# Bidirectional recurrence: score tiles side by side in PSUM, five double-width masked copies, diagonal products over 128 rows, keys on GpSimd

## The chip, the core and the metric

One Trainium2 chip, one of its cores, one launch. The metric is device time in microseconds of that core. Three timed runs of the kernel before gave 2304.19, 2304.97 and 4443.5 us; the median, 2304.97 us, is what a changed kernel is set against. The profile is of one further execution, which took 2300.62 us.

## What is computed

Two layers of a hybrid trunk over 512 latent tokens and 256 context tokens, width 1024. Each layer is a norm, one wide input projection, four token mixers, a gated merge, an output projection and an MLP. The change touches only the fourth mixer, a bidirectional gated recurrence (HGRN2) with 4 heads of 64 keys and 64 values. In one direction:

```python
def step(S, xs):                       # one chunk
    qc, kc, fc, ic = xs
    b = jnp.cumsum(fc, axis=2)         # running log decay
    diff = b[:, :, :, None, :] - b[:, :, None, :, :]
    dec = jnp.where(lower_tri, jnp.exp(jnp.minimum(diff, 0.0)), 0.0)
    a = jnp.einsum('bhtd,bhsd,bhtsd->bhts', qc, kc, dec)
    o = jnp.einsum('bhts,bhsv->bhtv', a, ic) + jnp.einsum('bhtd,bhdv->bhtv', qc * jnp.exp(b), S)
    return advance(S, b, kc, ic), o
```

It is run forwards and, on flipped tokens, backwards, and both results are added. Layer 0 needs it for all 768 tokens, layer 1 for the 512 latent tokens.

## The kernel before

Everything is written once in Python and put in order by a scheduler that knows priorities and its own cost of each instruction. The result is one fixed list of instructions for each engine, run in that order: an engine whose next instruction is not ready waits, whatever stands behind it.

Most of the time is dense work: a 128-row weight unit is loaded by DMA, split into a high and a low part (line 69 on ScalarE, `whi`; line 70 on VectorE, `wlo`), and multiplied in three products (lines 88, 89, 91, `big<-hhi,whi` and so on).

The recurrence works feature-major: the 64 keys of a head lie on partitions 0 to 63 for the forward direction and on 64 to 127 for the backward one, tokens along the free axis, in chunks of 128 tokens. `hg_state` (lines 438 to 479) makes the state of each chunk: decayed keys `hke`, a transpose on TensorE (line 457), a product with the values (line 463), and a running update `hs` on VectorE (line 477).

`hg_out` (from line 481) makes the outputs for two tiles of 128 tokens at a time; here such a pair of tiles is called a granule. Layer 0 has 4 heads x 3 granules, layer 1 has 4 x 2, so 20 granules in all. One granule is:

- `hE` (four VectorE subtractions, then two passes of ScalarE over 1024 columns): the decay to a reference point at four block sizes `LEVELS` of 64, 32, 16 and 8 tokens.
- `hKL`, the keys times `hE` for each level (line 503; levels 0 and 1 on GpSimd, 2 and 3 on VectorE), and `hQ`, the queries times `hE`, one VectorE instruction over 1024 columns.
- `hd`, `hem`, `hec`: the decay inside blocks of 8 tokens, times the queries (`hd`) and keys (`hem`), and the decay from the chunk's start, times the queries (`hec`).
- for each of the two tiles: four score products (line 525) over 128 rows, and two diagonal products over 64 rows each, the forward direction on rows 0 to 63 (line 526), the backward one on rows 64 to 127 (line 527). They land in two PSUM tiles (`sm`), and six masked copies on VectorE (lines 531 and 532, 128x128 each) put them together into two matrices A1 and A2 (`hA`).
- for each of the two tiles three output products (line 542): the state times `hec`, the values times A1, the values times A2. The two tiles use the two column halves of the array (`tile_position=(0, 64 * j)`), then ScalarE copies the output out (line 544).

`self.fill(n)` draws dense work (a quarter of a gate unit a time) from a generator, so that TensorE has something to do between the steps of a granule. PSUM tiles named `sm` rotate through four buffers, `hKL` and the pairs of `hA` through two each.

Of the kernel before, what the change touches and what calls it, by code (L numbers as in the profile page):

```python
# [8 lines left out]
F32 = mybir.dt.float32  # L9
# [4 lines left out]
AF = mybir.ActivationFunctionType  # L14
ALU = mybir.AluOpType
# [4 lines left out]
P = 128  # L20
# [30 lines left out]
class K:  # L51
# [429 lines left out]
    def hg_out(self, hd, S, grans, o, p, p2):  # L481
        nc = self.nc
        k, c, q = self.hk[hd], self.hc[hd], self.hq[hd]
        r0 = 64 * (hd % 2)
        G = 256
        for g in grans:
            a = g * G
            cs, qs_, ks = c[:, a:a + G], q[:, a:a + G], k[:, a:a + G]
            E = p.tile([P, 4, G], F32, name="hE")
            QL = p2.tile([P, 4, G], F32, name="hQ")  # L490
            for n, H in enumerate(LEVELS):
                nb = G // (2 * H)
                cv = cs.rearrange("p (b s) -> p b s", s=2 * H)
                self.tt(E[:, n].rearrange("p (b s) -> p b s", s=2 * H), cv,
                        cv[:, :, H:H + 1].to_broadcast([P, nb, 2 * H]), ALU.subtract)
            self.act(E, E, AF.Abs)
            self.act(E, E, AF.Exp, scale=-1.0)
            KL = self.hKL[self.kl_i % 2]
            self.kl_i += 1
            for n, H in enumerate(LEVELS):  # L500
                v = lambda t: t.rearrange("p (b s) -> p b s", s=2 * H)
                for lo_, hi_, h0 in ((0, 64, 0), (64, 128, H)):
                    (nc.vector if n >= 2 else nc.gpsimd).tensor_tensor(v(KL[lo_:hi_, n])[:, :, h0:h0 + H], v(ks)[lo_:hi_, :, h0:h0 + H],
                            v(E[lo_:hi_, n])[:, :, h0:h0 + H], ALU.mult)
            self.tt(QL, E, qs_[:, None, :].to_broadcast([P, 4, G]), ALU.mult)
            d = p2.tile([P, G], F32, name="hd")
            em = p2.tile([P, G], F32, name="hem")
            ec = p2.tile([P, G], F32, name="hec")
            self.fill(1)
            c8 = cs.rearrange("p (b s) -> p b s", s=8)  # L510
            self.tt(d.rearrange("p (b s) -> p b s", s=8), c8, c8[:, :, 4:5].to_broadcast([P, G // 8, 8]), ALU.subtract)
            self.act(em, d, AF.Exp, scale=-1.0)
            self.act(d, d, AF.Exp)
            self.act(ec, cs, AF.Exp)
            self.tt(d, d, qs_, ALU.mult)
            self.tt(em, em, ks, ALU.mult)
            self.tt(ec, ec, qs_, ALU.mult)
            sets = []
            for j in range(2):
                s = slice(j * P, (j + 1) * P)  # L520
                pa = self.p_sm.tile([P, 512], F32, name="sm")
                pb = self.p_sm.tile([P, 512], F32, name="sm")
                dst = [pa[:, 0:128], pa[:, 128:256], pa[:, 256:384], pb[:, 0:128], pa[:, 384:512], pb[:, 128:256]]
                for n in range(4):
                    nc.tensor.matmul(dst[n], KL[:, n, s], QL[:, n, s], start=True, stop=True)  # L525
                nc.tensor.matmul(dst[4], em[0:64, s], d[0:64, s], start=True, stop=True)
                nc.tensor.matmul(dst[5], em[64:128, s], d[64:128, s], start=True, stop=True)
                A1, A2 = self.hA[self.a_i % 2]
                self.a_i += 1
                for n in range(5):  # L530
                    nc.vector.copy_predicated(A1, self.masks[:, n], dst[n])
                nc.vector.copy_predicated(A2, self.masks[:, 5], dst[5])
                sets.append((A1, A2))

            self.fill(1)
            po = self.p_sm.tile([P, 512], F32, name="sm")
            for n in range(3):
                for j in range(2):
                    t = 2 * g + j
                    iv = self.hi_[:, t, hd * 64:hd * 64 + 64]  # L540
                    w, x = ((S[:, t], ec[:, j * P:(j + 1) * P]), (iv, sets[j][0]), (iv, sets[j][1]))[n]
                    nc.tensor.matmul(po[64 * j:64 * j + 64, 0:P], w, x, start=n == 0, stop=n == 2, tile_position=(0, 64 * j))  # L542
            for j in range(2):
                nc.scalar.copy(o[r0:r0 + 64, a + j * P:a + (j + 1) * P], po[64 * j:64 * j + 64, 0:P])

    def hg_begin(self, p, p1):
        nc = self.nc
        self.hk, self.hc, self.hq = {}, {}, {}
        self.kl_i = self.a_i = 0
        self.smask = p.tile([P, 384], U8, name="smask")  # L550
        m32 = p1.tile([P, T], F32, name="hge")[:, :384]
        nc.scalar.dma_start(m32, self.io["smask"])
        nc.vector.tensor_copy(self.smask, m32)
        self.hKL = [p.tile([P, 4, 256], F32, name=f"hKL{i}") for i in range(2)]
        self.hA = [[p.tile([P, P], F32, name=f"hA{i}{j}") for j in range(2)] for i in range(2)]
        for t in self.hKL:
            nc.gpsimd.memset(t, 0.0)
        for x in self.hA:
            for t in x:
                nc.gpsimd.memset(t, 0.0)  # L560
# [988 lines left out]
```

## Time and profile before

| | |
|---|---|
| median of three timed runs | 2304.97 us |
| the profiled execution | 2300.62 us |
| span from its first to its last instruction | 2298.8 us |
| TensorE matmul busy | 2232.7 us (97%) |
| VectorE busy | 1487.9 us (65%) |
| ScalarE busy | 940.7 us (41%) |
| GpSimd busy | 171.1 us (7%) |

An engine counts as busy from the start of an instruction to its end. Matmuls overlap: one that begins every 0.11 us is recorded with 0.27 us, so for TensorE the distance between two starts tells what a product costs, and the idle time in front of one tells what it waited for. A 4-byte product is recorded as two passes, so eight products of line 525 stand as x16.

### The profile page before, as it was taken

The page shows a single profiled execution, that of the slowest core. Times are in us where ns is not written, and L with a number is a line of the kernel's source. Part 1 is how long each engine was busy: PE and PEld are TensorE (multiplying, and loading weights), DVE is VectorE, ACT ScalarE, POOL GpSimd, SP SyncE. Part 2 cuts the span into 40 slices and gives each one's busy share as a digit, 9 for nine tenths or more (in the row PEclk, how much of TensorE's full clock was granted, in tenths as well). Part 3 has the DMA queues.
Part 4 walks back from the last instruction along what each step waited for, and adds up shares of the span by engine and source line. Part 5 has one row for each costly group of instructions (what it writes and reads, how often), then busy time and mean ns, then how long its engine had stood idle before and what let it go on. Part 6 is the DMA issues. An engine that isn't in the chain of part 4 may idle for free.

```text
span 2298.8 us, 32096 instructions
## 1 busy us (share of the span) xinstructions
PE 2232.7 (97%) x12642; PEld 1871.5 (81%) x12642; DVE 1487.9 (65%) x2754; ACT 940.7 (41%) x1664; POOL 171.1 (7%) x206
## 2 busy tenths in 40 slices
PE   6999999999999999999999999989999999999999
PEld 4878777888888888888888887776778888888887
DVE  6896967678983567655555568788866636544544
ACT  5554545445541342222222245464646524333231
POOL 0010100111112000000000000110111120000000
PEclk9999999999999999999999999999999999999999
DMA  7211110134343404333333322111122123323332
GB/s 276 79 38 49 35 62 19 47 106 158 122 160 105 146 29 137 120 111 118 118 114 127 101 91 78 56 56 62 47 69 95 65 92 128 101 93 101 93 100 83
DMA packets 64982, 217.58 MB, mean 95 GB/s; under 512 B 7936, under 2 KB 9856, under 8 KB 64576
## 3 DMA queue, kind: packets, MB, share of 16 engines
q1 hardware_dynamic: 63232, 210.16, 28.0%
q0 software_dynamic: 1024, 2.88, 0.5%
q10 hardware_dynamic: 576, 2.49, 0.3%
q8 instruction: 99, 1.62, 0.3%
q14 instruction: 51, 0.42, 0.1%
HBM read 210.27 MB, written 5.24 MB: 94 GB/s over the span
## 4 chain that ended last, share of the span: by engine, by line
PE 84%; DVE 9%; ACT 3%; issue 2%; DMA 1%; POOL 0%; SPq 0%; DVEq 0%; ACTq 0%; POOLq 0%
PE big L89 23%; PE big L88 23%; PE big L91 22%; PE sm L731 2%; PE sm L764 2%; PE sm L525 2%; DVE wlo L70 2%; DVE hgc L395 1%; PE sm L776 1%; PE sm L89 1%; PE sm L88 1%; PE sm L91 1%; PE sm L542 1%; PE sm L923 1%; ACT whi L69 1%
## 5 line engine op out<-in xcount | busy, mean ns | idle before, releaser
L88 PE MATMUL big<-hhi,whi 128*128 128x512 f32 (+1 forms) x1928 | 689.6, 358 | 5.7 <-ACT hhi L156 3.7
L89 PE MATMUL big<-hlo,whi 128*128 128x512 f32 (+1 forms) x1928 | 687.7, 357 | 1.0 <-DVE hlo L360 0.9
L91 PE MATMUL big<-hhi,wlo 128*128 128x512 f32 (+1 forms) x1928 | 686.0, 356 | 2.4 <-DVE wlo L70 2.4
L69 ACT CAST whi<-raw 128x1024 fp32r<-128x1024 f32 (+1 forms) x268 | 279.2, 1045 | 845.0 <-PE big L89 798.9
L70 DVE TENSOR_TENSOR wlo<-raw,whi 128x1024 fp32r<-128x1024 f32 (+1 forms) x268 | 331.0, 1238 | 363.1 <-ACT whi L69 358.9
L88 PEld LDWEIGHTS big<-hhi,whi 128*128 128x128 f32 x1928 | 365.3, 190 | 61.2 <-ACT hhi L156 5.0
L91 PEld LDWEIGHTS big<-hhi,wlo 128*128 128x128 f32 x1928 | 365.6, 190 | 54.8 <-DVE wlo L70 3.1
L89 PEld LDWEIGHTS big<-hlo,whi 128*128 128x128 f32 x1928 | 366.0, 190 | 53.7 <-issue 3.4
L89 PE MATMUL big<-flo,whi 128*128 128x512 f32 (+1 forms) x744 | 265.5, 357 | 0.0
L88 PE MATMUL big<-fhi,whi 128*128 128x512 f32 (+1 forms) x744 | 265.3, 357 | 0.0
L91 PE MATMUL big<-fhi,wlo 128*128 128x512 f32 (+1 forms) x744 | 264.8, 356 | 0.0
L1223 DVE SCALAR_TENSOR_TENSOR xr<-big,mods,xr 128x256 f32<-128x256 f32 (+1 forms) x205 | 131.1, 663 | 198.6 <-PE big L91 198.2
L88 PEld LDWEIGHTS big<-fhi,whi 128*128 128x128 f32 x744 | 140.6, 189 | 20.7
L91 PEld LDWEIGHTS big<-fhi,wlo 128*128 128x128 f32 x744 | 140.4, 189 | 20.4
L89 PEld LDWEIGHTS big<-flo,whi 128*128 128x128 f32 x744 | 140.7, 189 | 20.1
L1060 POOL TENSOR_TENSOR m<-m,gg 128x768 f32<-128x768 f32 (+1 forms) x48 | 87.4, 1826 | 575.7 <-DVE gg L1058 443.7
L313 DVE CUSTOM_DVE_ANT_0 adaj<-raw,crow 128x1024 bf16<-128x1024 f32 x64 | 80.4, 1256 | 16.5 <-DMA raw<-in_ada_b_w_dram 15.6
L313 DVE CUSTOM_DVE_ANT_0 adaj<-adar,crow 128x1024 bf16<-128x1024 f32 x64 | 78.1, 1220 | 0.5
L88 PE MATMUL big<-yhi,whi 128*128 128x512 f32 x192 | 69.0, 359 | 0.0
L89 PE MATMUL big<-ylo,whi 128*128 128x512 f32 x192 | 68.9, 359 | 0.0
L91 PE MATMUL big<-yhi,wlo 128*128 128x512 f32 x192 | 68.4, 356 | 0.0
L156 ACT ACTIVATE mpk<-sm,sxm,krt 128x512 f32<-128x512 f32 (+1 forms) x72 | 46.9, 657 | 45.9 <-DVE sxm L713 38.4
(311 smaller groups left out, 3350.7 us busy)
## 6 DMA issues: line engine op xcount, KB each, us to landing
raw<-in_w_ff_dram SPq DMA_DIRECT2D x128, 512.0 KB, 3.5
raw<-in_w_cm_dram SPq DMA_DIRECT2D x98, 512.0 KB, 3.3
adar<-in_ada_b_w_dram SPq DMA_DIRECT2D x48, 512.0 KB, 3.4
raw<-in_ada_b_w_dram SPq DMA_DIRECT2D x32, 512.0 KB, 3.3
adaw<-in_ada_a_dram SPq DMA_DIRECT2D x16, 512.0 KB, 7.6
raw<-in_w_br_dram SPq DMA_DIRECT2D x16, 512.0 KB, 3.5
raw<-in_w_out_dram SPq DMA_DIRECT2D x16, 512.0 KB, 3.5
nbias<-in_nab_dram SPq DMA_DIRECT2D x8, 384.0 KB, 4.0
```

Source lines behind the costliest of these rows:

```text
L69: nc.scalar.copy(hi[:, :n], raw[:, :n])
L70: nc.vector.tensor_tensor(lo[:, :n], raw[:, :n], hi[:, :n].bitcast(F32), ALU.subtract)
L88: mm(out, w.hi[:, kt], rhs.hi[:, kt, t0:t0 + n], start=start, stop=False)
L89: mm(out, w.hi[:, kt], rhs.lo[:, kt, t0:t0 + n], start=False, stop=False)
L91: self.last_mm = mm(out, w.lo[:, kt], rhs.hi[:, kt, t0:t0 + n], start=False, stop=stop).ins
L156: self.nc.scalar.activation(out, in_, f, **kw)
L313: nc.vector.tensor_tensor_reduce(junk, w, self.srow[:, v], 1.0, 0.0, ALU.mult, ALU.add, x[:, v:v + 1])
L525: nc.tensor.matmul(dst[n], KL[:, n, s], QL[:, n, s], start=True, stop=True)
L731: nc.tensor.transpose(pt[:, (kt - a) * P:(kt - a + 1) * P], pk[:, kt * P:(kt + 1) * P], self.ident)
L764: nc.tensor.matmul(ps[:, 0:b - a], qx[:, qr], kx[:, a:b], start=i == 0, stop=i == 2)
L1060: nc.gpsimd.tensor_tensor(m, m, g, ALU.add)
L1223: self.last_v = nc.vector.scalar_tensor_tensor(x, ps[:, po:po + n], self.mods[l][:, gate + d, v:v + 1], x, ALU.mult, ALU.add).ins
```

## The change

All in `hg_out` and `hg_begin`, lines 481 to 563:

- the two tiles of a granule lie side by side: six score kinds go to three PSUM tiles, each with two kinds x two tiles x 128 columns, and a masked copy now covers both tiles (128x256). There are five of them (line 535 of the changed kernel) in place of twelve.
- the coarsest kind (level 64) is not copied by mask but by two ScalarE copies of 64 rows x 2 x 64 columns (line 533); what its mask selects is just these two blocks.
- the diagonal products run over 128 rows (line 527 with the others): their keys are kinds 4 and 5 of a widened `hKL`, whose other 64 rows are zero.
- these keys are made by two ScalarE exponentials of 64 rows and two GpSimd products of 64x256 (line 515), in place of one exponential and one VectorE product of 128x256 (`hem`, gone).
- the output products (line 545) are written with the values first and the state last.
- `hKL` grows by half, `hA` doubles, and the scratch space of DMAs issued by GpSimd is set to 8192 bytes.

```diff
-            em = p2.tile([P, G], F32, name="hem")
...
-            self.act(em, d, AF.Exp, scale=-1.0)
+
+            for n, lo_ in ((4, 0), (5, 64)):
+                r = slice(lo_, lo_ + 64)
+                self.act(KL[r, n], d[r], AF.Exp, scale=-1.0)
+                nc.gpsimd.tensor_tensor(KL[r, n], KL[r, n], ks[r], ALU.mult)
             self.act(d, d, AF.Exp)
             self.act(ec, cs, AF.Exp)
             self.tt(d, d, qs_, ALU.mult)
-            self.tt(em, em, ks, ALU.mult)
             self.tt(ec, ec, qs_, ALU.mult)
-            sets = []
-            for j in range(2):
-                s = slice(j * P, (j + 1) * P)
-                pa = self.p_sm.tile([P, 512], F32, name="sm")
-                pb = self.p_sm.tile([P, 512], F32, name="sm")
-                dst = [pa[:, 0:128], pa[:, 128:256], pa[:, 256:384], pb[:, 0:128], pa[:, 384:512], pb[:, 128:256]]
-                for n in range(4):
-                    nc.tensor.matmul(dst[n], KL[:, n, s], QL[:, n, s], start=True, stop=True)
-                nc.tensor.matmul(dst[4], em[0:64, s], d[0:64, s], start=True, stop=True)
-                nc.tensor.matmul(dst[5], em[64:128, s], d[64:128, s], start=True, stop=True)
-                A1, A2 = self.hA[self.a_i % 2]
-                self.a_i += 1
-                for n in range(5):
-                    nc.vector.copy_predicated(A1, self.masks[:, n], dst[n])
-                nc.vector.copy_predicated(A2, self.masks[:, 5], dst[5])
-                sets.append((A1, A2))
+
+            dst = []
+            for i in range(3):
+                ps = self.p_sm.tile([P, 512], F32, name="sm").rearrange("p (n j s) -> p n j s", n=2, j=2)
+                for n in (2 * i, 2 * i + 1):
+                    for j in range(2):
+                        s = slice(j * P, (j + 1) * P)
+                        nc.tensor.matmul(ps[:, n % 2, j], KL[:, n, s], QL[:, n, s] if n < 4 else d[:, s], start=True, stop=True)
+                    dst.append(ps[:, n % 2])
+            A1, A2 = self.hA[self.a_i % 2]
+            self.a_i += 1
+
+            for lo_, h0 in ((0, 64), (64, 0)):
+                nc.scalar.copy(A1[lo_:lo_ + 64, :, h0:h0 + 64], dst[0][lo_:lo_ + 64, :, h0:h0 + 64])
+            for n in range(1, 6):
+                nc.vector.copy_predicated(A1 if n < 5 else A2, self.masks[:, n, None].to_broadcast([P, 2, P]), dst[n])
...
-                    w, x = ((S[:, t], ec[:, j * P:(j + 1) * P]), (iv, sets[j][0]), (iv, sets[j][1]))[n]
+                    w, x = ((iv, A2[:, j]), (iv, A1[:, j]), (S[:, t], ec[:, j * P:(j + 1) * P]))[n]
...
-    nc = _bacc.Bacc("TRN2", target_bir_lowering=False, num_devices=1)
+    nc = _bacc.Bacc("TRN2", target_bir_lowering=False, num_devices=1, dynamic_dma_scratch_size=8192)
```

The scheduler orders the work anew. On TensorE this is the second granule of layer 0's first head in the order before, from its score products to its output products (names end in a buffer number; the output side comes in two pieces with dense rows between):

```order
L525 MATMUL sm<-hQ,hKL_710 128x128 x4
L526 MATMUL sm<-hd,hem 128x128
L527 MATMUL sm<-hd,hem 128x128
L525 MATMUL sm<-hQ,hKL_710 128x128 x4
...
L542 MATMUL sm<-hec,hs 64x128 x2
L542 MATMUL sm<-hA_711,hgi 64x128
...
L542 MATMUL sm<-hA_713,hgi 64x128
L542 MATMUL sm<-hA_712,hgi 64x128
L542 MATMUL sm<-hA_714,hgi 64x128
```

The same granule on TensorE in the changed kernel, dense rows left out between scores and outputs:

```order
L527 MATMUL sm<-hQ,hKL_710 128x128 x8
L527 MATMUL sm<-hd,hKL_710 128x128 x4
...
L545 MATMUL sm<-hA_714,hgi 64x128 x2
L545 MATMUL sm<-hA_713,hgi 64x128 x2
L545 MATMUL sm<-hec,hs 64x128 x2
```

The switches to 64-row products inside the score block are gone, and the output products stand in one piece. In the whole order before, 15 of the 20 score blocks have the pattern 4, 2, 4, 2 shown, one has 7, 2, 1, 2 and four have 8, 4; 19 of the 20 output sides are split. Afterwards all 20 are 8, 4 (one of them with dense rows between) and no output side is split. Between the last score product and the first output product stand 5 to 19 rows, ten in the middle.

On VectorE the same granule's masked copies before are twelve of 128x128, those of the two tiles mixed (here from the fourth to the eighth; `hA00` and `hA01` belong to the first tile, `hA10` and `hA11` to the second, the last number is that of the PSUM tile):

```order
L531 COPY_PREDICATED hA10_713<-c_mask8_583,sm_1323 128x128
L531 COPY_PREDICATED hA00_711<-c_mask8_583,sm_1310 128x128
L532 COPY_PREDICATED hA01_712<-c_mask8_583,sm_1310 128x128
L531 COPY_PREDICATED hA00_711<-c_mask8_583,sm_1309 128x128
L531 COPY_PREDICATED hA10_713<-c_mask8_583,sm_1323 128x128
```

In the changed kernel they are these five, with what stands between them, and on to the next granule's `hQ`:

```order
L535 COPY_PREDICATED hA10_713<-c_mask8_583,sm_1305 128x256
L153 TENSOR_TENSOR hd_1379<-hgc_723 128x256
L535 COPY_PREDICATED hA10_713<-c_mask8_583,sm_1310 128x256
L153 TENSOR_TENSOR hec_1380<-hec_1380,hgq_804 128x256
L535 COPY_PREDICATED hA10_713<-c_mask8_583,sm_1310 128x256
L153 TENSOR_TENSOR hke_1452<-hke_1452,hgk_866 128x256
L535 COPY_PREDICATED hA10_713<-c_mask8_583,sm_1315 128x256
L535 COPY_PREDICATED hA11_714<-c_mask8_583,sm_1315 128x256
...
L70 TENSOR_TENSOR wlo_1384<-raw_1381,whi_1383 128x1024
...
L153 TENSOR_TENSOR hQ_1363<-hE_1362,hgq_804 128x1024
```

The five copies replace twelve, and up to three other instructions stand between the first and the last of a granule. On GpSimd the new key products stand behind the level products of the same or the next buffer; these are three granules in the middle of layer 0:

```order
L515 TENSOR_TENSOR hKL_709<-hKL_709,hgk 64x256 x2
L503 TENSOR_TENSOR hKL_709<-hgk,hE 64x2x64 x2
L503 TENSOR_TENSOR hKL_709<-hgk,hE 64x4x32 x2
L515 TENSOR_TENSOR hKL_710<-hKL_710,hgk 64x256 x2
L503 TENSOR_TENSOR hKL_710<-hgk,hE 64x2x64 x2
```

Two rows are added to every four there. The rest of the program keeps its order on every engine but for some rows of the attention that follows the recurrence in layer 1.

## Rows read from the trace of the kernel before

**Rows 1.** Page, part 4: the chain that ended last, shares by engine
```profile
PE 84%; DVE 9%; ACT 3%; issue 2%; DMA 1%; POOL 0%; SPq 0%; DVEq 0%; ACTq 0%; POOLq 0%
```
**Rows 2.** Recurrence stages: length, then PE, PEld, DVE, ACT, POOL busy, clock, DMA
```profile
85.00:305.00 220.00, 208.19 (x1333) 173.17 (x1333) 180.47 (x435) 114.01 (x210) 24.30 (x55) 0.99 0.13 42
1390.00:1580.00 190.00, 178.35 (x1029) 142.36 (x1028) 153.58 (x355) 105.12 (x194) 16.66 (x39) 1.00 0.19 61
```
**Rows 3.** Groups by form: busy us, mean ns | idle before, releaser
```profile
L525 PE MATMUL sm<-hQ,hKL 128*128 128x128 f32 x320 | 43.9, 282 | 5.3 <-DVE hQ L153 5.3
...
L526 PE MATMUL sm<-hd,hem 64*128 64x128 f32 x80 | 18.4, 317 | 1.9 <-DVE hd L153 1.3 <-DVE hem L153 0.6
...
L457 PE MATMUL sm<-c_ident,hke 128*128 128x128 f32 x48 | 10.0, 292 | 9.8 <-DVE hke L153 9.8
...
L542 PE MATMUL sm<-hec,hs 128*64 128x128 f32 x80 | 8.8, 298 | 0.5 <-DVE hA L532 0.5
```
**Rows 4.** Timeline, TensorE, a score block: start us, us, engine, instruction
```profile
169.34 1.06 PE L525 MATMUL sm<-hQ,hKL 128*128 128x128 f32 x8
170.32 0.37 PE L526 MATMUL sm<-hd,hem 64*128 64x128 f32 x1
...
170.53 0.27 PE L526 MATMUL sm<-hd,hem 64*128 64x128 f32 x1
...
170.74 1.16 PE L525 MATMUL sm<-hQ,hKL 128*128 128x128 f32 x8
...
172.25 0.50 PE L88 MATMUL big<-hhi,whi 128*128 128x512 f32 x1
```
**Rows 5.** Timeline, TensorE, eight 128-row score products without a switch
```profile
1527.91 2.02 PE L525 MATMUL sm<-hQ,hKL 128*128 128x128 f32 x16 [0.89 <-DVE hQ L153]
1529.69 0.48 PE L88 MATMUL big<-hhi,whi 128*128 128x512 f32 x1
```
**Rows 6.** Timeline, TensorE, first piece of a split output side
```profile
174.21 0.40 PE L91 MATMUL big<-hhi,wlo 128*128 128x512 f32 x1
174.53 0.44 PE L542 MATMUL sm<-hec,hs 128*64 128x128 f32 x4
...
175.11 0.50 PE L88 MATMUL big<-hhi,whi 128*128 128x512 f32 x1
175.45 0.39 PE L89 MATMUL big<-hlo,whi 128*128 128x512 f32 x1
175.68 0.40 PE L91 MATMUL big<-hhi,wlo 128*128 128x512 f32 x1
```
**Rows 7.** Timeline, TensorE, the one output side in one piece
```profile
183.33 0.44 PE L542 MATMUL sm<-hec,hs 128*64 128x128 f32 x4
...
184.14 0.50 PE L88 MATMUL big<-yhi,whi 128*128 128x512 f32 x1
```
**Rows 8.** Timeline, VectorE: masked copies, subtractions, key products
```profile
144.81 0.56 DVE L503 TENSOR_TENSOR hKL<-hgk,hE 64x128 f32<-64x128 f32 x1
...
145.61 0.29 DVE L503 TENSOR_TENSOR hKL<-hgk,hE 64x128 f32<-64x128 f32 x1
...
166.00 1.09 DVE L153 TENSOR_TENSOR hE<-hgc 128x256 f32<-128x256 f32 x3
...
1533.19 1.09 DVE L531 COPY_PREDICATED hA<-c_mask,sm 128x128 f32<-128x128 uint8 x5
```
**Rows 9.** Groups by form: GpSimd and ScalarE work of a granule
```profile
L503 POOL TENSOR_TENSOR hKL<-hgk,hE 64x128 f32<-64x128 f32 x80 | 38.5, 481 | 335.2 <-ACT hE L156 292.5 <-DVE hA L531 17.4 <-DVE hA L532 7.3
...
L544 ACT COPY ho<-sm 64x128 f32<-64x128 f32 x40 | 10.4, 259 | 21.4 <-PE sm L542 20.7
...
L156 ACT ACTIVATE hem<-hd 128x256 f32<-128x256 f32 x20 | 7.9, 409 | 1.3 <-DVE hd L153 1.2
```
**Rows 10.** Line 857 (GpSimd's DMA) and line 923, its reader: ns min/median/max, starts
```profile
L857 POOL DMA_DIRECT2D nv<-vperm x2: 762/762/762, 546.5 to 1761.9; - x2
...
L923 PE MATMUL sm<-nPT,nv x288: 272/273/324, 569.8 to 1827.1; 128*64 128x128 f32 x144
```

More of the change, by code (lines that the diff above doesn't have):

```diff
@@ L553, in hg_begin @@
         nc.vector.tensor_copy(self.smask, m32)
-        self.hKL = [p.tile([P, 4, 256], F32, name=f"hKL{i}") for i in range(2)]
-        self.hA = [[p.tile([P, P], F32, name=f"hA{i}{j}") for j in range(2)] for i in range(2)]
+        self.hKL = [p.tile([P, 6, 256], F32, name=f"hKL{i}") for i in range(2)]
+        self.hA = [[p.tile([P, 2, P], F32, name=f"hA{i}{j}") for j in range(2)] for i in range(2)]
         for t in self.hKL:
```

## The prediction

> **What bounds the kernel now.** I read the chain of work that ended last first: 84% of it runs through TensorE and 9% through VectorE [rows 1]. So for the program as a whole a microsecond of TensorE time saved is a microsecond won, and a microsecond saved elsewhere counts only where TensorE waits for it.
>
> Then the two stages in which the recurrence runs, by windows [rows 2]. They are 220 and 190 us long, 410 of 2298.8 us, so the rest of the program is out of the change's reach. In them TensorE is busy for 208.2 and 178.4 us and idle for 11.8 and 11.7 us. VectorE is busy for 180.5 of 220 and 153.6 of 190 us, over 80%: it is the second limit here. ScalarE stands at 114.0 and 105.1 us and GpSimd at 24.3 and 16.7 us, both with room.
>
> Then the groups by form, for whom TensorE waits [rows 3]. Score products waited 5.3 us for `hQ`, diagonal products 1.9 us for `hd` and `hem`, and the transposes of `hg_state`, which the change does not touch, 9.8 us for `hke`. All three are late work of VectorE. That gives two ways to win: fewer microseconds of TensorE in the granules (certain to count), and up to 7.2 + 9.8 = 17.0 us of waits.
>
> **Score products on TensorE.** Their number stays at twelve a granule; four of them grow from 64 to 128 rows. Eight 128-row products take 1529.69 - 1527.91 = 1.78 us from the first start to the next work, 0.222 us each [rows 5]; twelve in a row would take 2.67 us. The block of before, four, two, four, two, takes 172.25 - 169.34 = 2.91 us [rows 4]. Its rows show why it is not shorter: the two 64-row products of a pair do start together, but the pair's two passes stand 0.21 us apart (170.32, 170.53, then 170.74 for the next work), where passes of 128-row products stand 0.11 us apart (1.78 us for sixteen). One pair so costs 0.42 us, against 0.44 us for two full products, and the following pass start is late as well. The gain is 0.24 us a block. It holds for the 16 blocks that go back and forth twice; the four that do it once I count at nothing. 16 x 0.24 = 3.8 us.
>
> Here a rule speaks against the change. The Trainium skill, TensorEngine Tiling (Array Packing), Overview, says that products with at most 64 contracted rows can run two at a time as row tiles, up to twice as fast; giving that up would cost two products of 0.222 us a granule, 20 x 0.44 = 8.9 us lost in place of 3.8 us won. The same page, Key Properties, says that a change of tiling mode drains the engine, and the gaps of 0.21 us in [rows 4] agree with that: with single pairs between full products the one eats up the other. The trace decides, and I take 3.8 us won.
>
> **Output products on TensorE.** Before, 19 of 20 granules issue them in two pieces with dense work between; afterwards all are whole. A piece of three products takes 175.11 - 174.53 = 0.58 us, and it delays its surroundings: it starts 0.32 us after the dense product ahead of it and the second dense product behind starts 0.34 us after the first, where neighbours stand 0.23 us apart [rows 6]. That makes 0.58 + 0.09 + 0.11 = 0.78 us, twice 1.56 us. The one granule in one piece takes 184.14 - 183.33 = 0.81 us [rows 7], with the same edges 1.01 us: in one piece the products of both tiles run in pairs throughout, in pieces of three one is alone. 19 x (1.56 - 1.01) = 10.5 us. TensorE saves 3.8 + 10.5 = 14.3 us in all, 0.72 us a granule.
>
> **VectorE.** Five masked copies in a row are recorded with 1.09 us and three subtractions of 256 columns with 1.09 us too [rows 8]. Taking the last one's overlap off (about 0.1 us), a 128-column copy costs 0.20 us and a 256-column instruction 0.33 us. No row has a 256-column masked copy; its bounds are 0.20 (nothing for width) and 0.40 us (two old ones), and I take 0.33. Then 12 x 0.20 = 2.40 us become 5 x 0.33 = 1.65 us, and `hem` takes 0.33 us with it: 1.08 us saved a granule (bounds 0.73 and 1.73).
>
> Some of it goes back. A key product on GpSimd costs 0.48 us for 128 columns [rows 9]; for 256 the bounds are 0.48 and 0.96, and I take 0.72, so 1.44 us more of GpSimd a granule. Two like VectorE instructions, one beside GpSimd work and one not, take 0.56 and 0.29 us [rows 8]: VectorE loses up to half its speed meanwhile. If all 1.44 us fell on such instructions that would cost 0.7 us, if on copies out of PSUM nothing by the rows; I take half, 0.35 us. The Trainium skill, GPSIMD Engine Reference, Key points, states the sharing of SBUF access with VectorE that this looks like, for instructions with two SBUF inputs. VectorE keeps 1.08 - 0.35 = 0.7 us a granule. TensorE's blocks shrink by as much (0.72 us), so neither gets ahead of the other, and I leave the waits of [rows 3] as they are. Their bounds: all 17.0 us gone, or as much again.
>
> **Edits at nothing.** ScalarE gets one more exponential (0.41 us; at half the rows no less, at most the same) and two copies like that of line 544 (0.26 us each): 0.93 us a granule [rows 9], 11 and 7 us in stages where it has 106 and 85 us free. The keys on GpSimd stand behind four level products, 4 x 0.48 + 2 x 0.72 = 3.4 us after `hE` is there. What hides them: VectorE has two to four key products and `hQ` to make from the same `hE`, and TensorE then has eight products (1.78 us) before the first that reads the new keys. With 0.29 us a key product and 1.2 us for `hQ` (four times the columns of a 0.33 us one, less its fixed part) that is some 3.6 us at the least. If the cover is gone, each late key costs TensorE its own 0.72 us. The smaller scratch space can only delay the twenty DMAs of GpSimd; the last ones of layer 0 are issued at 546.5 us and first read at 569.8 us [rows 10], with over 20 us between.
>
> **The new wait.** Outputs now stand behind all five copies of both tiles. From the first score product: 0.89 us until the first PSUM tile is full, 0.52 us for ScalarE's copies, 1.65 us for VectorE's, with four hand-overs of some 0.1 us about 3.5 us. TensorE has 2.67 us of scores and then about ten dense rows of 0.12 to 0.23 us (256 and 512 columns), together about 4.6 us. The 1.1 us left hold the up to three other instructions (0.33 us each) that now stand between the copies. So nothing, as long as VectorE comes to the first copy in time.
>
> **Sum.** 2300.6 - 14.3 = 2286.3 us for an execution like the profiled one, which was 4.4 us below the median of the three runs shown. On the median's scale 2305.0 - 14.3 = 2290.7; I forecast 2291 us.
>
> **Rivals**, on the same scale.
> *The waits go too.* If VectorE's saving is worth more than TensorE's, the 7.2 us at the scores and half of the 9.8 us at the transposes go: 2290.7 - 12.1 = 2279 us. For it speaks that all three waits are for VectorE; against it, that the list of rows is planned anew and the planner fills the gap it expects. Chance 0.22.
> *The gain turns into waits.* Where VectorE sets a granule's pace, a shorter TensorE block only lengthens the wait at the next score block. If VectorE saves nothing (bounds 0.73, less 0.7 for GpSimd's company), some 2 us remain: 2303 us. Against it: TensorE is busy for 94% of these stages, so it waits in few granules. Chance 0.17.
> *The pairs were cheap.* If a pair of 64-row products costs the time of one full product, two products of 0.222 us a granule are lost, 8.9 us, and 10.5 - 8.9 = 1.6 us remain: 2303 us. Against it stand the 0.42 us of a pair [rows 4]. Chance 0.04. It is the rule of TensorEngine Tiling (Array Packing) in the Trainium skill, without its clause on the drain.
> *Slower: outputs wait for the copies.* The place is the first output product behind the fifth copy. If VectorE comes to the first copy 2.4 us late, by one `hQ` and one `wlo` (1.2 us each, both 1024 columns) queued ahead, the 1.1 us reserve is gone and 1.3 us a granule are lost, 26 us: 2305.0 - 14.3 + 26 = 2317 us. It decides from 0.72 us a granule upward, that is a delay of 1.8 us. For it: the `wlo` in the rows shown ahead of `hQ`. Against it: the six copies of the first tile already bind the outputs now, and they were waited for 0.5 us in all [rows 3]. Chance 0.10.
>
> **Numbers.** The forecast has a chance of 0.43 with its own range 2284 to 2298 us (copy and key prices at their bounds, 3 us of waits either way); 0.04 is left for anything larger. To hold 8 in 10 the range takes in the first three rivals but not the slower one: 2275 to 2304 us. Faster or slower by over 2%, 46 us (about what a measurement of this kernel can tell from no change), is out of reach of every case above: 0.02 and 0.03, and 0.95 for within 2%.
>
> **What would show it.** Right: score blocks of about 2.67 us and output blocks of 0.8 us, 20 of each, and TensorE's busy time down by about 14 us; masked copies 0.3 us apart; waits for `hQ` still near 5 us. Wrong: score blocks above 2.9 us (the rule on row tiles); idle time over 10 us before line 545, released by line 535 (the slower rival); idle before line 527 released by GpSimd's line 515 (keys late); waits for `hQ` over 15 us with busy time down all the same (gain turned into waits).

## The result, and the profile after

The changed kernel takes 2322.07 us in the median (2315.47 to 2323.27), the kernel before beside it 2304.74 us: a ratio of 1.0072, with an interval of 1.006 to 1.0084. It is slower by 0.7%, where 0.6% faster was forecast; 2322 us lies outside the range.

The engines' busy time and the recurrence stages of the changed kernel, the page's part 1 and the windows of [rows 2]:

```profile
PE 2227.7 (96%) x12642; PEld 1881.7 (81%) x12642; DVE 1485.6 (64%) x2594; ACT 959.2 (41%) x1724; POOL 213.0 (9%) x246
```
```profile
85.00:305.00 220.00, 194.57 (x1258) 168.98 (x1259) 172.96 (x330) 120.47 (x237) 46.10 (x78) 0.97 0.12 39
1390.00:1580.00 190.00, 172.35 (x985) 143.18 (x984) 153.43 (x289) 111.09 (x215) 34.54 (x56) 0.97 0.20 63
```

TensorE's busy time went from 2232.7 to 2227.7 us, by 5 us and not by 14; its idle time rose from 66.1 to 86.0 us (span less busy time). In the stages idle time is now 25.4 and 17.7 us where it was 11.8 and 11.7 [rows 2]. GpSimd's work in the two stages doubled (46.1 and 34.5 us against 24.3 and 16.7). VectorE was to lose 14 us of work and lost 2.3 (1487.9 to 1485.6).

The groups by form (busy us, mean ns | idle before, releaser), to be read beside [rows 3] and [rows 9]:

```profile
L535 DVE COPY_PREDICATED hA<-c_mask,sm 128x256 f32<-128x256 uint8 x100 | 42.1, 443 | 20.0 <-ACT hA L533 17.2 <-PE sm L527 0.4
L527 PE MATMUL sm<-hQ,hKL 128*128 128x128 f32 x320 | 41.8, 286 | 10.5 <-DVE hQ L153 10.5
L515 POOL TENSOR_TENSOR hKL<-hKL,hgk 64x256 f32<-64x256 f32 x40 | 39.0, 975 | 30.4 <-ACT hKL L156 18.6 <-DVE hec L153 9.7
...
L503 DVE TENSOR_TENSOR hKL<-hgk,hE 64x128 f32<-64x128 f32 x80 | 35.4, 442 | 6.9 <-ACT hE L156 5.9
...
L527 PE MATMUL sm<-hd,hKL 128*128 128x128 f32 x160 | 22.0, 282 | 2.5 <-DVE hd L153 2.5
...
L545 PE MATMUL sm<-hA,hgi 128*64 128x128 f32 x160 | 13.2, 284 | 12.6 <-DVE hA L535 12.2 <-ACT hKL L156 0.3
...
L457 PE MATMUL sm<-c_ident,hke 128*128 128x128 f32 x48 | 10.6, 304 | 14.0 <-DVE hke L153 13.9
```

The four waits of TensorE in this stage add up to 14.0 + 10.5 + 2.5 + 12.6 = 39.6 us; before they were 9.8 + 5.3 + 1.9 + 0.5 = 17.5. Nearly all of it is put down to VectorE. The largest new one stands before the output products, 12.2 us for the masked copies.

How it comes about is seen in the first granule of layer 0. The timeline of the changed kernel, all engines (start us, us, engine, instruction, idle before it):

```profile
117.95 3.04 DVE L153 TENSOR_TENSOR hE<-hgc 128x256 f32<-128x256 f32 x4
118.10 2.60 POOL L515 TENSOR_TENSOR hKL<-hKL,hgk 64x256 f32<-64x256 f32 x3 [2.62 <-ACT hKL L156]
...
119.60 2.00 PE L527 MATMUL sm<-hQ,hKL 128*128 128x128 f32 x16
...
121.58 2.46 DVE L477 SCALAR_TENSOR_TENSOR hs<-hs,hdd 64x64 f32<-64x64 f32 x8
...
122.16 0.53 ACT L533 COPY hA<-sm 64x128 f32<-64x128 f32 x2
...
124.08 1.00 DVE L535 COPY_PREDICATED hA<-c_mask,sm 128x256 f32<-128x256 uint8 x2
...
125.93 0.77 DVE L535 COPY_PREDICATED hA<-c_mask,sm 128x256 f32<-128x256 uint8 x2
...
126.85 0.66 PE L545 MATMUL sm<-hA,hgi 128*64 128x128 f32 x8 [2.05 <-DVE hA L535]
```

Three key products on GpSimd run from 118.10 to 120.70, and beside them VectorE's four subtractions take 3.04 us, where three took 1.09 before [rows 8], so four about 1.45. VectorE is 1.6 us late from there on, and the head's eight state steps (`hs`, 2.46 us) still stand ahead of the masked copies in its list. ScalarE's copies are done at 122.69; VectorE comes to the first masked copy only at 124.08, and TensorE, done with its filling work, waits 2.05 us.

The trace shows the same in other granules. In ten of the twenty VectorE comes to the first copy 0.6 to 4.0 us after ScalarE's last, and these ten hold 10.8 of the 12.6 us of waits before the outputs; six of them, with 9.2 us, have the state's eight steps just ahead of the copies.

The second loss is the clock. A score block behind a long wait in the changed kernel (timeline of TensorE), the windows' row inside it, and an undisturbed block:

```profile
248.21 2.98 PE L527 MATMUL sm<-hQ,hKL 128*128 128x128 f32 x16 [3.70 <-DVE hQ L153]
250.97 1.78 PE L527 MATMUL sm<-hd,hKL 128*128 128x128 f32 x8
252.50 0.48 PE L88 MATMUL big<-hhi,whi 128*128 128x512 f32 x1
```
```profile
249.10:252.50 3.40, 3.40 (x19) 3.40 (x18) 2.80 (x9) 0.52 (x2) 0.00 (x0) 0.50 0.45 154
```
```profile
181.07 1.95 PE L527 MATMUL sm<-hQ,hKL 128*128 128x128 f32 x16
182.85 1.06 PE L527 MATMUL sm<-hd,hKL 128*128 128x128 f32 x8
183.66 0.36 PE L88 MATMUL big<-hhi,whi 128*128 128x256 f32 x1
```

The block takes 252.50 - 248.21 = 4.29 us at a granted clock of 0.50 (1.2 GHz, the lower level) and 183.66 - 181.07 = 2.59 us undisturbed. Leaving out the start and the end of the program, the trace shows 30.7 us at the lower level in the changed kernel and 6.8 us before; in the changed kernel each such stretch begins within 1.4 us of the end of a TensorE wait of 1.6 to 4.3 us. At half clock a stretch does half its work (the block above lost 4.29 - 2.59 = 1.70 us in 3.40 us of it), so 23.9 us more of it can cost up to 12 us. This time differs from one execution of a kernel to the next: those of the kernel before had mean granted clocks from 0.992 (2308 us) to 0.997 (2299 us), and its profiled one stands at 0.997.

That closes the account of the two profiled executions, 2313.7 - 2298.8 = +14.9 us: TensorE's blocks, taken as forecast, -14.3; busy time that was not won in spite of it, 14.3 - 5.1 = +9.2, which the lower clock can explain; the four waits, 39.6 - 17.5 = +22.1; all other idle time of TensorE -2.2.

### The profile page after: what moved, and what is told of

It reads as the page before. It is cut to its first block, busy times and chain, and to the rows that moved or that the text cites. A ratio compares the mean times of both kernels' runs of the same rounds, so it can differ in the third digit from the quotient of the medians.

```text
span 2313.7 us, 32138 instructions
## 1 busy us (share of the span) xinstructions
PE 2227.7 (96%) x12642; PEld 1881.7 (81%) x12642; DVE 1485.6 (64%) x2594; ACT 959.2 (41%) x1724; POOL 213.0 (9%) x246
## 3 DMA queue, kind: packets, MB, share of 16 engines
q0 software_dynamic: 1024, 2.88, 0.5%
## 4 chain that ended last, share of the span: by engine, by line
PE 80%; DVE 13%; ACT 3%; issue 3%; DMA 1%; POOL 0%; SPq 0%; DVEq 0%; ACTq 0%; POOLq 0%
PE big L89 22%; PE big L88 22%; PE big L91 22%; PE sm L734 2%; DVE wlo L70 2%; PE sm L767 2%; PE sm L527 1%; DVE hKL L503 1%; PE sm L779 1%; PE sm L89 1%; PE sm L88 1%; PE sm L91 1%; DVE hgc L395 1%; DVE hA L535 1%; DVE hs L477 1%
```

## Experiments

Three theories. **A**: GpSimd's products slow VectorE's own instructions, VectorE comes late, and TensorE waits. **B**: ScalarE's copies, set between TensorE's scores and VectorE's masked copies, are a hop too many. **C**: output products that stand behind the copies of both tiles come too early, whatever makes the keys. A later rival, **E**: the keys arrive late from GpSimd.

The runs of this study, to be looked up from the sections below. Times are medians, with the ratio to the kernel before on the same chip (its medians were 2303.7 to 2304.7 us). "Waits" is the sum of the four groups above; "low clock" the time at the lower level without start and end; both, like the busy and idle times, are of one execution each. "Loss" is worked out from the trace, to about 1.5 us: for each kind of VectorE instruction, the time of those that ran beside a GpSimd product of this stage, less their number times the median of those that did not.

| kernel | us | ratio | PE busy | PE idle | waits | low clock | DVE busy | loss |
|---|---|---|---|---|---|---|---|---|
| before | 2304.7 | 1 | 2232.7 | 66.1 | 17.5 | 6.8 | 1487.9 | 12.9 |
| changed | 2322.1 | 1.006–1.0084 | 2227.7 | 86.0 | 39.6 | 30.7 | 1485.6 | 32.6 |
| keys on VectorE | 2302.9 | 0.9992–1.0011 | 2221.0 | 79.6 | 30.2 | 13.7 | 1483.1 | 13.8 |
| coarse kind by mask | 2315.5 | 1.0037–1.007 | 2228.8 | 84.2 | 36.1 | 30.7 | 1492.4 | 33.2 |
| both undone | 2300.0 | 0.9981–1.0 | 2222.2 | 74.6 | 25.2 | 13.7 | 1490.1 | 15.3 |
| before, `hem` on GpSimd | 2314.7 | 1.0038–1.0068 | 2240.5 | 71.3 | 23.0 | 20.5 | 1490.0 | 20.7 |
| 64-row pairs | 2297.2 | 0.9964–0.9982 | 2224.3 | 71.7 | 23.6 | 17.1 | 1470.7 | 12.9 |
| pairs, six masks | 2297.3 | 0.9961–0.9983 | 2225.1 | 71.3 | 23.6 | 17.1 | 1478.0 | 12.8 |
| both undone, fill moved | 2297.8 | 0.9968–0.9986 | 2219.7 | 74.9 | 25.7 | 10.2 | 1489.1 | 14.1 |
| before, level keys on VectorE | 2311.8 | 1.002–1.0047 | 2240.9 | 67.7 | 17.2 | 27.3 | 1497.0 | 0 |
| pairs, six masks, fill moved | 2297.1 | 0.9955–0.998 | 2225.9 | 67.3 | 19.3 | 20.5 | 1476.7 | 12.2 |
| pairs, fill moved | 2293.5 | 0.994–0.9965 | 2226.0 | 65.7 | 19.4 | 23.9 | 1471.0 | 13.4 |
| changed, fill moved | 2317.3 | 1.0041–1.0071 | 2229.5 | 87.4 | 39.5 | 34.1 | 1487.8 | 34.1 |
| keys on VectorE, idle products | 2317.1 | 1.0045–1.0072 | 2229.9 | 87.6 | 38.2 | 30.7 | 1496.6 | 27.5 |

### The keys back on VectorE

```diff
-                nc.gpsimd.tensor_tensor(KL[r, n], KL[r, n], ks[r], ALU.mult)
+                nc.vector.tensor_tensor(KL[r, n], KL[r, n], ks[r], ALU.mult)
```

> The changed kernel with one part undone: the two key products of 64x256 (line 515) run on VectorE in place of GpSimd. In the changed kernel VectorE instructions beside GpSimd's products lose 32.6 us, before the change 12.9 us. Theory A (GpSimd's keys slow VectorE, whose delay becomes TensorE's waits): VectorE gets 20 us back and pays 20 x 2 x 0.33 = 13 us; the waits before score, transpose and output products fall from about 39 us to under 28 us, the half-clock stretches from nine to five or fewer, and the time comes to 2300 to 2310 us. Theory B (the extra hop through ScalarE ahead of the first masked copy makes the waits): no gain, 2318 to 2330 us, VectorE still idles about 17 us before line 535. Theory C (outputs now stand behind the copies of both tiles, whoever makes the keys): 2315 to 2325 us, with the waits before the output products near 12 us.

2302.9 us: 19 us come back by this line alone, though VectorE takes on 40 products. Its loss beside GpSimd falls from 32.6 to 13.8 us, about as before the change (12.9). But 12.7 us of waits more than before remain, and they eat TensorE's 11.7 us. By groups:

```profile
L527 PE MATMUL sm<-hQ,hKL 128*128 128x128 f32 x320 | 40.0, 278 | 8.4 <-DVE hQ L153 8.4
...
L545 PE MATMUL sm<-hA,hgi 128*64 128x128 f32 x160 | 13.2, 283 | 9.0 <-DVE hA L535 8.8
L457 PE MATMUL sm<-c_ident,hke 128*128 128x128 f32 x48 | 10.1, 292 | 11.9 <-DVE hke L153 11.7
```

So A accounts for the slowdown, and something else for the gain that does not show: the outputs still wait 9.0 us. The trace shows where: 5.9 us in granules where VectorE has the state's steps to do just ahead of the masked copies, 2.2 us in one where it has four level products and a `hQ`. So VectorE is late there by the order of its list, without the keys on GpSimd.

### The coarsest kind by a sixth masked copy, and both undone

```diff
-            for lo_, h0 in ((0, 64), (64, 0)):
-                nc.scalar.copy(A1[lo_:lo_ + 64, :, h0:h0 + 64], dst[0][lo_:lo_ + 64, :, h0:h0 + 64])
-            for n in range(1, 6):
+            for n in range(6):
```

> The changed kernel with another part undone: the coarsest kind is a sixth masked copy of 128x256 on VectorE; ScalarE's two copies of line 533 are gone. Theory A (GpSimd's keys): VectorE gets 20 x 0.33 = 7 us more work and nothing back, so 2320 to 2330 us. Theory B (the hop through ScalarE): the 17 us in which VectorE idles behind line 533 shrink below 7 us, the waits before the output products fall from 12.6 to under 6 us, time 2303 to 2313 us. Theory C (both tiles' copies ahead of the outputs): 2318 to 2328 us, output waits unchanged or longer by 0.3 us a granule.

> The changed kernel with both parts undone: keys on VectorE and the coarsest kind by a sixth masked copy. What is left of the change is the side-by-side layout, the 128-row diagonal products and the order of the output products. Theory A alone: like the version with keys on VectorE alone plus 0 to 7 us for the sixth copy. Theory B alone: like the version with the masked coarsest kind plus up to 13 us. Both: under 2300 us, the 14 us saved on TensorE then show at last. Theory C: 2310 us or more, output waits above 8 us.

With the keys left on GpSimd 2315.5 us, with both undone 2300.0 us: 6.6 and 2.9 us less than with ScalarE's copies. The first lies in none of the three ranges (A from 2320, B to 2313, C from 2318 us), the second below what A alone gave and at the edge of "both". B explains less than half of the loss of 17 us. Without the hop the masked copies still wait, now for TensorE's scores in place of ScalarE's copies, and the outputs wait as long as before it was taken out (groups of the first of the two kernels):

```profile
L533 DVE COPY_PREDICATED hA<-c_mask,sm 128x256 f32<-128x256 uint8 x120 | 50.9, 441 | 14.2 <-PE sm L527 12.2
...
L543 PE MATMUL sm<-hA,hgi 128*64 128x128 f32 x160 | 13.1, 284 | 13.0 <-DVE hA L533 11.8 <-ACT whi L69 1.1
```

### The kernel before with its one key product on GpSimd

```diff
-            self.tt(em, em, ks, ALU.mult)
+            nc.gpsimd.tensor_tensor(em, em, ks, ALU.mult)
```

> The kernel before with one part of the change alone: the key product hem of 128x256 is made by GpSimd. Theory A (GpSimd beside VectorE costs VectorE about half of GpSimd's time): 20 products of some 0.75 us cost VectorE 7 to 9 us and save it 20 x 0.33 = 7 us; a later key for the diagonal products adds waits; 2303 to 2313 us and VectorE's loss beside GpSimd up from 12.9 to about 21 us. Theories B and C: nothing but the 7 us saved on VectorE matters, 2297 to 2305 us.

2314.7 us, 1.7 us above A's range and far above that of B and C. One part of the change alone, put into the kernel before, makes it 0.5% slower: A without B and C. VectorE gives away 8.6 us of `hem`, as recorded, and its busy time still rises by 2.1 us, as its loss rises by 7.8. The diagonal products, which read the key, waited 4.6 us against 1.9, all of it for VectorE's `hd`. That VectorE's total hardly changes and 10 us are lost all the same says that the place counts: waits rise by 5.5 us and time at the lower clock by 13.7. GpSimd's product, 0.33 us forecast for VectorE, takes 956 ns there:

```profile
L516 POOL TENSOR_TENSOR hem<-hem,hgk 128x256 f32<-128x256 f32 x20 | 19.0, 956 | 51.7 <-ACT hem L156 13.6 <-DVE hA L532 10.4 <-DVE hs L477 10.3
```

### The same products on GpSimd, read by nobody

The kernel with the keys on VectorE, and beside each key product a like one on GpSimd into a tile of its own:

```diff
                 nc.vector.tensor_tensor(KL[r, n], KL[r, n], ks[r], ALU.mult)
+                nc.gpsimd.tensor_tensor(self.hx[r], KL[r, n], ks[r], ALU.mult)
```

> The changed kernel with the key products on VectorE (2302.86 us), and with the same 40 products of 64x256 once more on GpSimd, into a tile that nothing reads. Nobody waits for GpSimd's results here, so only what they do to VectorE's own instructions is left. Theory A: VectorE's instructions beside them are about doubled again, its loss rises from 14 to about 30 us, stretches at half clock rise again, and the time is 2314 to 2324 us. Rival E (the keys arrive late from GpSimd, and that is the loss): no change, 2302 to 2305 us.

2317.1 us, as A gave, 14.2 us more than without them. No engine waits for these products, and the score products, which read the level keys that GpSimd makes between them, wait 8.4 us as without them, so rival E (late keys) can't be the reason: their company alone costs this. VectorE's busy time rises by 13.5 us, its loss by 13.7. The groups show where; `hd` took 430 ns on average without them:

```profile
L516 POOL TENSOR_TENSOR hx<-hKL,hgk 64x256 f32<-64x256 f32 x40 | 34.8, 870 | 86.6 <-DVE hKL L515 85.6
...
L153 DVE TENSOR_TENSOR hd<-hd,hgq 128x256 f32<-128x256 f32 x20 | 13.6, 680 | 0.4
...
L546 PE MATMUL sm<-hA,hgi 128*64 128x128 f32 x160 | 14.5, 305 | 14.8 <-DVE hA L536 12.7 <-ACT whi L69 1.9
```

### The kernel before without GpSimd in the stage

```diff
-                    (nc.vector if n >= 2 else nc.gpsimd).tensor_tensor(v(KL[lo_:hi_, n])[:, :, h0:h0 + H], v(ks)[lo_:hi_, :, h0:h0 + H],
+                    nc.vector.tensor_tensor(v(KL[lo_:hi_, n])[:, :, h0:h0 + H], v(ks)[lo_:hi_, :, h0:h0 + H],
```

> The kernel before, with its 80 level-key products of 64x128 (line 503, GpSimd, 38.5 us there) on VectorE, so that GpSimd does no product in this stage. At the 0.29 us that one of them takes on VectorE undisturbed, VectorE gets 23 us more work. Theory A (about half of GpSimd's time comes back as lengthening of VectorE's own instructions): VectorE's lines lose 12.9 us less, net 10 us more busy, and the time is 2304 to 2312 us, with median times of lines 503, 493 and 505 shorter by 5 to 15 per cent. Rival (products on GpSimd are free for VectorE, and the losses beside them have another cause): no line of VectorE gets shorter, busy time is up by 23 us or more and the time is 2312 to 2325 us.

2311.8 us, at the upper end of what A gave; busy time rose by 9.1 us and not by the 23 of the rival. Undisturbed, all 160 level products take 45.7 us on VectorE, 286 ns each. Before, VectorE's half of them took 31.7 us, 396 ns each, since GpSimd did the other half beside it. The 38.5 us of GpSimd [rows 9] so spared VectorE 9.1 us of busy time. The kernel is 7.8 us slower without them, but how the one becomes the other isn't shown: the four waits did not rise (17.2 us), and what the profiled execution lost stands in 20.5 us more at the lower clock, most of it outside the recurrence stages. The forecast that `hQ` and the subtractions would get 5 to 15% shorter too did not hold: 1281 to 1225 ns and no change. The level products on VectorE in the kernel before, then without GpSimd:

```profile
L503 DVE TENSOR_TENSOR hKL<-hgk,hE 64x128 f32<-64x128 f32 x80 | 31.7, 396 | 4.1 <-ACT hE L156 3.1
```
```profile
L503 DVE TENSOR_TENSOR hKL<-hgk,hE 64x128 f32<-64x128 f32 x160 | 45.7, 286 | 5.5 <-ACT hE L156 3.2
...
L477 DVE SCALAR_TENSOR_TENSOR hs<-hs,hdd 64x64 f32<-64x64 f32 x64 | 17.9, 280 | 2.0
```

### 64-row pairs in the merged block

Scores and outputs stay merged, but the diagonal kinds are made as before: one product `hem` of 128x256 on VectorE, and 64-row pairs, now all behind the sixteen full passes.

```diff
+            self.tt(em, em, ks, ALU.mult)
...
+                nc.tensor.matmul(dst[4][:, j], em[0:64, s], d[0:64, s], start=True, stop=True)
+                nc.tensor.matmul(dst[5][:, j], em[64:128, s], d[64:128, s], start=True, stop=True)
```

> The changed kernel with the diagonal kinds as in the kernel before (one 128x256 product of keys on VectorE, four 64-row products in a block of sixteen-product length), ScalarE's copies of the coarsest kind kept; scores and outputs stay merged. Theory A (GpSimd's two key products slow VectorE, and nothing else is lost): GpSimd's 39 us beside VectorE are gone and VectorE pays one product of 0.33 us a granule, 7 us, where the run with the keys on VectorE paid two halves; 2297 to 2303 us, waits on line 535's copies no longer than the 9.0 us of that run. Theory B (ScalarE's copies in front of the masked ones are the loss): still above 2305 us, since they are kept. Theory C (outputs that stand behind the copies of both tiles keep the gain whatever makes the keys): 2300 to 2303 us, with TensorE still idle 8 to 10 us before the output products. Rival D (the 128-row products were worth the forecast's 0.24 us a granule-half more than the pairs): score blocks longer by 0.2 us each and 2307 us.

> The kernel of the run before this one, with the coarsest kind under a sixth masked copy on VectorE and no copy on ScalarE. VectorE gets about 0.44 us a granule more, 9 us, and a hop from TensorE over ScalarE to VectorE goes. Theory A alone: VectorE's added work is partly seen, 2300 to 2306 us. Theory B: the hop was the longer, 2293 to 2298 us and idle before the outputs down to 4 us or less. Theory C: 2298 to 2302 us, idle before the outputs 8 us, as in the run that undid both.

2297.2 and 2297.3 us; both beat the kernel before. Against the keys on VectorE in two halves this is 5.7 us less, with 12.4 us less work for VectorE. Rival D falls: the score block is not longer but shorter, 181.85 - 179.32 = 2.53 us (timeline of TensorE) against 2.59 us of the changed kernel's block shown above.

```profile
179.32 1.95 PE L524 MATMUL sm<-hQ,hKL 128*128 128x128 f32 x16
181.20 0.37 PE L527 MATMUL sm<-hd,hem 64*128 64x128 f32 x1
181.21 0.37 PE L528 MATMUL sm<-hd,hem 64*128 64x128 f32 x1
181.41 0.27 PE L527 MATMUL sm<-hd,hem 64*128 64x128 f32 x1
...
181.53 0.27 PE L527 MATMUL sm<-hd,hem 64*128 64x128 f32 x1
...
181.85 0.39 PE L88 MATMUL big<-hhi,whi 128*128 128x256 f32 x1
```

In a run the passes of pairs stand 0.12 us apart, two products each; only the first and the last edge take 0.21 us. Of B little is left here: with and without ScalarE's copies the time is the same, though they spare VectorE 7.3 us, so the hop seems to cost about what it spares.

### The filling work moved to where the outputs wait

A piece of other TensorE work (`fill`) stands ahead of the scores, another between scores and outputs. The edit puts both there; it was made on four kernels.

```diff
             ec = p2.tile([P, G], F32, name="hec")
-            self.fill(1)
...
-            self.fill(1)
+            self.fill(2)
             po = self.p_sm.tile([P, 512], F32, name="sm")
```

> The kernel that undid both (keys on VectorE, six masked copies; 2300.0 us), with the piece of other TensorE work that was placed ahead of the scores moved between scores and outputs, where two pieces now stand. Nothing is computed otherwise. Theory C (the outputs stand behind the last masked copy, too close to it): TensorE's idle before the outputs falls from 8.0 to under 3 us, waits before the scores (7.2 and 0.9 us) grow by 0 to 4 us, and the time is 2292 to 2298 us. Rival (VectorE's chain from one granule to the next sets the rate, so a wait that goes at one place comes back at another): the sum of waits stays near 25 us and the time within 2 us of 2300.

> Merged scores and outputs, diagonal kinds as 64-row pairs with one product of keys on VectorE, six masked copies and none on ScalarE (2297.3 us), with the piece of other TensorE work moved from ahead of the scores to between scores and outputs. If the two gains add (the move brought 2300.0 to 2297.8 us where the keys were two products): 2293 to 2296 us, idle before the outputs down from 7.8 to about 5 us. If VectorE's chain sets the sum of waits: 2297 us, with the idle moved to the transposes and the scores (together 20 to 25 us).

> As the run before this one, with the coarsest kind copied by ScalarE again (the first of the merged runs with pairs, 2297.15 us, with the piece of other work moved). ScalarE's hop would stand under two pieces of other work: if it then costs nothing, 2292 to 2296 us, and no slower than the run before this one, since VectorE has 9 us less to do; if the hop is what stands last ahead of the outputs (theory B), idle there stays at 6 us or more and the time is 2297 us or above.

> The changed kernel itself, keys on GpSimd and the coarsest kind on ScalarE, with only the piece of other TensorE work moved to between scores and outputs. Theory A (GpSimd's products lengthen VectorE's instructions, and VectorE's chain sets the waits): idle before the outputs falls from 12.6 to 5 to 8 us, part of it comes back before the scores and the transposes, VectorE's loss beside GpSimd stays near 32 us, and the time is 2314 to 2320 us. Theory C (the place of the outputs is the loss, whatever makes the keys): 2300 to 2310 us.

On the kernel with both undone: 2300.0 to 2297.8 us. The outputs' wait fell from 8.0 to 5.5 us, the others took it up (the sum 25.2 to 25.7 us). The waits went as the rival on VectorE's chain has it, but the time lies in C's range (2292 to 2298 us) and just outside the rival's (2298 to 2302), so this run does not decide between them. On the changed kernel: 2317.3 us, as A gave and outside what C alone gave (2300 to 2310 us); waits stay at 39.5 us, VectorE's loss at 34.1, though the outputs' own wait fell only to 11.5 us where A had 5 to 8. On the pairs with six masks: nothing (2297.3 to 2297.1 us), though the sum of waits went from 23.6 to 19.3 us in the profiled execution; time at the lower clock rose by 3.4 us, and why the medians agree stays open. On the pairs with ScalarE's copies: 2293.5 us, in the range for a hop that costs nothing under the moved work, the fastest here, 0.35 to 0.6% faster than the kernel before. Its engines and groups:

```profile
PE 2226.0 (97%) x12642; PEld 1871.5 (82%) x12642; DVE 1471.0 (64%) x2614; ACT 949.8 (41%) x1704; POOL 172.7 (8%) x206
```
```profile
L523 PE MATMUL sm<-hQ,hKL 128*128 128x128 f32 x320 | 40.2, 279 | 5.6 <-DVE hQ L153 5.5
...
L544 PE MATMUL sm<-hA,hgi 128*64 128x128 f32 x160 | 15.6, 291 | 4.2 <-DVE hA L534 4.2
...
L457 PE MATMUL sm<-c_ident,hke 128*128 128x128 f32 x48 | 11.0, 303 | 9.0 <-DVE hke L153 9.0
```

VectorE does 16.9 us less than before, the waits are back at 19.4 us (17.5 before), and what is won on TensorE is seen in the time, less what 23.9 us at the lower clock take.

## Why the prediction was wrong

**TensorE's terms held.** Undisturbed score blocks take 2.59 to 2.67 us (2.67 forecast), nineteen output blocks 0.81 us in one piece and one, at the lower clock, 0.86. Busy time fell by 5 us only; with half of the time at the lower clock taken off on both sides, it fell by 17.0 us, and by 12.7 to 16.9 in the other ten kernels of the table with merged blocks. The reason given for the score block was only half right: it is shorter because it no longer goes back and forth, not because of 128 rows, as the pairs in a run show (2.53 us). The Trainium skill, TensorEngine Tiling (Array Packing), Overview, has it that products of at most 64 rows can run two at a time: in a run the trace agrees, 0.12 us a pass of two. The drain that its Key Properties name fits the 0.21 us at either edge. The rule was dismissed on single pairs.

**The step that failed is VectorE's sum**: "If all 1.44 us fell on such instructions that would cost 0.7 us, if on copies out of PSUM nothing by the rows; I take half, 0.35 us." A key product took 0.975 us on average, not 0.72, and above its upper bound of 0.96; 1.95 us of GpSimd a granule, not 1.44. And nearly all of it fell on instructions it slows (36 of the 40 products had VectorE instructions with two SBUF inputs beside them for over 85% of their time): the loss rose by 32.6 - 12.9 = 19.7 us, 0.99 a granule, above the bound of 0.7. The other terms of that sum held, as busy time: without GpSimd's part the pairs with fill moved save 16.9 us, 0.85 a granule by the copies alone (0.75 forecast). VectorE kept 2.3 us in all, 0.12 a granule, not 0.7. By this alone the rival "the gain turns into waits" (2303 us) was to come true, and the run with the keys on VectorE, which spares VectorE 4.8 us, shows it at 2302.9 us.

**The new wait was not nothing.** The reserve of 1.1 us a granule was worked out for a VectorE that comes to the first copy in time, and for copies of 1.65 us. Five with nothing between them take 2.36 us:

```profile
174.86 2.36 DVE L535 COPY_PREDICATED hA<-c_mask,sm 128x256 f32<-128x256 uint8 x5 [1.09 <-ACT hA L533]
```

The four into the first matrix each start after the one before has ended (0.47 to 0.56 us apart), where those of [rows 8], 0.20 us apart, went to several matrices in turn. So 0.4 us of reserve was left. VectorE was 1.4 us late in the granule shown (124.08 against 122.69), as its subtractions took 3.04 us, and the copies, with key products between them, stretched over 2.6 us. The sign named for the slower rival, over 10 us before line 545 released by line 535, is there: 12.2 us. The rival (2317 us) had the place right and the cause in part: work queued ahead of the copies, but mostly the state's steps and not a `hQ` and a `wlo`, on a VectorE that was slowed besides. Both rivals were taken as alternatives; they share VectorE's lateness, and came together.

**What was missing**: a price for waits beyond their own length. Behind some of them TensorE ran at the lower clock, up to some 9 us in the profiled execution that stand in no term of the sum.

**At nothing**: ScalarE's added work was 18.5 us, 0.93 a granule, as forecast. But its copies are a step of the chain and were not free: VectorE idled 17.2 us for them, and without them the time is 6.6 us less (keys on GpSimd) or 2.9 us (keys on VectorE). Keys that came late cost nothing that the trace shows: four weight loads that idled 10.3 us are put down to line 515, but each of its products had ended 1.2 to 2.4 us before that load ran, and TensorE's products there waited for VectorE's `hQ` or `hd`.

## What to carry to other kernels

Work moved to GpSimd from a VectorE that sets the pace must be priced with what it takes from VectorE's neighbours: here 39 us moved took 20 us back, and the waits that followed cost more than TensorE had won. Before outputs of several tiles are put behind one set of copies, ask how late the copying engine can be, what its list puts ahead of the copies, and whether each copy must wait for the one before; and move other work there to cover it. Where two rivals hang on the same engine's lateness, price them together.

## What the chip showed that was not expected

- Short VectorE instructions with two inputs in SBUF about double beside GpSimd products: in the changed kernel the subtractions for `hE` 0.418 us alone and 0.816 beside, the state's steps (`hs`) 0.281 and 0.609. The longer `hQ` went from 1.225 to 1.504, and masked copies out of PSUM don't change (0.443 and 0.440). The Trainium skill, GPSIMD Engine Reference, Key points, names the sharing; its size is from these rows.
- GpSimd's time varies too: a 64x256 product took 0.72 us at the least and 1.75 at the most. The nine longest, 1.58 us and more, all ran beside a `hQ` or a `wlo` of 1024 columns, but others beside a `hQ` took 0.72, and why isn't shown.
- Twice the columns of a masked copy out of PSUM cost 0.44 against 0.30 us, half as much again, and a copy into the matrix of the one before starts only after that one's end.
- Time at the lower clock did not go in step with the waits: in the profiled executions the fastest kernel has 23.9 us of it, the kernel before 6.8, and the one without GpSimd in the stage 27.3 with no more waits.
